# One-hot gate matrices stored by pairs of tokens instead of by eights

## The chip, the cores and the metric

One NeuronCore of a Trainium2 chip runs the whole program; the other cores are idle. The metric is the device time of one execution in microseconds (us), median of three executions. TensorE (PE; its weight loads are listed as PEld), VectorE (DVE), ScalarE (ACT), GpSimd (POOL) and the DMA queue engine (SP) run side by side, each taking its own instructions strictly in order and waiting on semaphores of the others.

## What is computed

One decoder layer over 512 tokens of width 1024: an attention head group, a state-space head group, and at the end an expert mixer, which is where this change lies. For each token 8 heads choose 16 of 16,384 experts each; expert number e = 128·i1 + i2:

```
eidx = take_along_axis(i1 * 128 + i2, sel)      # 8 heads x 16 experts per token
gate = softmax(top)
hid  = einsum('bcd,bchkd->bchk', xb, u_tab[eidx])
act  = gelu(hid) * gate
out  = einsum('bchk,bchkd->bcd', act, v_tab[eidx])
```

Then a residual sum and a last RMS norm.

## The kernel before

The 512 tokens are four tiles of 128. Tiles 0 and 1 ("sparse") gather the rows of their chosen experts from memory, 128 rows at a time. Tiles 2 and 3 ("dense", together 256 tokens) don't gather: they go through all 16,384 experts in 128 blocks of 128 (`dense`, loop over j), multiply every expert with every token, and weight the result with a gate that is zero where the token did not choose the expert. That needs, for each of the 256 tokens, a 128 x 128 table of gates (i1 by i2).

**How a gate table is made.** `dtab` holds for each token, on 128 partitions (one for each of its 8 x 16 choices), four f16 numbers: i1, i2, the gate's high part and its low part. `gate_parts(c, t0, b0)` treats eight tokens t0 to t0+7 at once and one half c of the i2 values (JC = 64 of them). It has four parts, separated by `yield`:

1. DVE writes A: for every token a 128 x 128 one-hot matrix of i1 (128 x 1024 numbers on 128 partitions, f16).
2. DVE writes B0, the one-hot matrix of the half of i2 (128 x 512), and then B, which is B0 times the high part (q = 0) and B0 times the low part (q = 1), 128 x 1024 together.
3. PE: for each token two matmuls (q = 0 and 1) with A as stationary and B as moving operand, 64 columns each, summed into one PSUM bank: 16 weight loads and 16 matmuls for eight tokens.
4. ACT copies the bank (128 x 512) into the gate rows in SBUF.

So A is built as `[i1, token]` with the eight tokens innermost, and PE reads one token of it with a step of 16 bytes; B likewise. `io8` is the constant that DVE compares with: the numbers 0 to 127, each eight times.

**Where it runs.** 32 groups with c = 0 run ahead of the loop over j, by `gate_tokens`, right after the first block's `hi`, `lo`, `hid` and `gelu`. This text calls that stretch the gate stage. Its buffers come from six small slots, three for a group (B0, A, B), so that two groups can be under way. A slot's freeing order makes a group's B0 and A lie where A and B of the group two before it lay. The order of the instructions in this stretch is not written by hand: the builder's scheduler interleaves the groups with each other and with their neighbours. The 32 groups with c = 1 run inside the loop, one for every two blocks up to about block 62; there the order on DVE, ACT, PE and POOL is as written (`with ordered(...)`), and B0 lies in `junk`, which the next `dot` overwrites.

One block of the loop: `hi` (ACT) and `lo` (DVE) split the loaded expert rows into two parts; `hid` (24 matmuls of 256 columns) and `outp` (12 of 512) on PE; `gelu` and `acthi` on ACT; `gated` and `actlo` on DVE; and one step of tile 1's gather work (`dot` and `add` on DVE, 128 x 1024 each). All instructions pass through one recording helper, so the profile names line 134 for nearly all of them, and tiles have to tell them apart: `X` is the large SBUF arena, `XH`/`XL` the split tokens, `bank` a PSUM bank.

Of the kernel before, what the change touches and what calls it, by code (L numbers as in the profile page):

```python
# [15 lines left out]
F16 = mybir.dt.float16  # L16
# [3 lines left out]
ALU = mybir.AluOpType  # L20
# [11 lines left out]
JC = 64  # L32
# [111 lines left out]
def both(g1, g2, n):  # L144

    for x in g1:
        yield x
        for _ in range(n):
            next(g2, None)
    yield from g2  # L150
# [7 lines left out]
def paced(w, g):  # L158
    for _ in g:
        yield w  # L160
# [3 lines left out]
def hymba_kernel(ctx: ExitStack, tc: tile.TileContext, a, out, dbg=None):  # L164
    nc = tc.nc
    pins = set()
    V, S, G, PE = (Ordered(tc, e, n, pins) for e, n in ((nc.vector, "V"), (nc.scalar, "S"), (nc.gpsimd, "G"), (nc.tensor, "PE")))
# [22 lines left out]
    base = arena.tile([128, 32768], F32, name="X")  # L190
# [6 lines left out]
    def bank():  # L197
        return pool[0].popleft()

    def bfree(*bs):  # L200
        pool[0].extend(bs)
# [88 lines left out]
    def load_w(name, n, pref=(4, 5)):  # L290
        r = [M.L(pref) for _ in range(2)]
        for i in range(2):
            SP.dma_start(r[i].v([128, 4, n]), a[name][:, 4 * i:4 * i + 4])
        return r, lambda k: r[k // 4].v([128, 4, n])[:, k % 4]
# [7 lines left out]
    w2 = const("w2", [128, 2, 64])  # L302
    msl = M.L((3,))
    VC = msl.v([128, NT, 280])
    io8 = msl.v([128, 128, 8], F16)
    dtab = msl.v([128, 4, 256], F16, off=4480)
    cmpb = msl.v([128, NT, 2, 31], off=7040)
    SP.dma_start(cmpb, a["cmpb"])
# [272 lines left out]
    def proj_q(T, w, e):  # L581
        p = bank()
        proj(T, w, 512, p)
        qs, ts = M.S(), M.S()
        Q = qs.v([128, 8, 64])
        S.activation(qs.v([128, 512]), p, AF.Copy, scale=0.125)
        bfree(p)
        rope_apply(e, Q, 8, ts.v([128, 8, 16]), ts.v([128, 8, 16], off=512), rope[:, T, 0], rope[:, T, 1])
        p = bank()
        for i in range(4):  # L590
            PE.transpose(b3(p, 128)[:, i], Q[:, 2 * i:2 * i + 2].rearrange("p h d -> p (h d)"), ident)
        S.activation(qT[T], b3(p, 128), AF.Copy)
        bfree(p)
        M.free(qs, ts)
        tap(f"qT{T}", qT[T])

    def proj_k(T, w, e):
        p = bank()
        proj(T, w, 512, p)
        ks_, ts = [M.S(), M.S()], M.S()  # L600
        KD = [k.v([128, 4, 2, 64]) for k in ks_]
        for i in range(2):
            S.activation(KD[i][:, :, 0], b3(p, 64)[:, 4 * i:4 * i + 4], AF.Copy)
        S.activation(KD[1][:, :, 1], b3(p, 64)[:, 4:8], AF.Copy)
        bfree(p)
        rope_apply(e, KD[0][:, :, 0], 4, ts.v([128, 4, 16]), ts.v([128, 4, 16], off=512), rope[:, T, 0], rope[:, T, 1])
        S.activation(KD[0][:, :, 1], KD[0][:, :, 0], AF.Copy)
        t0 = T * 128
        for n in (1, 0):
            p = bank()  # L610
            pv = b3(p, 128)
            for i in range(4):
                PE.transpose(pv[:, i], KD[n][:, i].rearrange("p u d -> p (u d)"), ident)
            if n == 0:
                S.activation(KT[:, :, t0:t0 + 128], pv, AF.Copy)
            else:
                S.activation(CTv[0:64, :, t0:t0 + 128], pv[0:64], AF.Copy)
                S.activation(CTv[64:128, :, max(t0 - 1, 0):t0 + 127], pv[64:128, :, 1 if T == 0 else 0:], AF.Copy)
            bfree(p)
        M.free(*ks_, ts)  # L620

    def proj_c(T, w):
        p = bank()
        proj(T, w, 280, p)
        S.activation(VC[:, T], p[:, 0:280], AF.Copy)
        bfree(p)
# [3 lines left out]
    def gates(T0, T1):  # L630

        g = gts[:, T0:T1]
        S.activation(g, VC[:, T0:T1, 256:280].rearrange("p t (h b) -> p t h b", b=3), AF.Tanh, scale=0.5)
        V.tensor_scalar(g, g, 1.0, 0.5, op0=ALU.add, op1=ALU.mult)
# [535 lines left out]
    def row(r):  # L1170
        return base[:, 2048 * (4 + r):2048 * (5 + r)]
# [13 lines left out]
    def gate_parts(c, t0, b0):  # L1185

        al, bl = M.S(), M.S()
        A = al.v([128, 128, 8], F16)
        B0 = Slot(b0, "B").v([128, JC, 8], F16)
        B = bl.v([128, 2, JC, 8], F16)  # L1190
        tsl = slice(t0, t0 + 8)
        V.tensor_tensor(A, io8, dtab[:, 0, None, tsl].to_broadcast([128, 128, 8]), op=ALU.is_equal)
        yield
        V.tensor_tensor(B0, io8[:, c * JC:(c + 1) * JC], dtab[:, 1, None, tsl].to_broadcast([128, JC, 8]), op=ALU.is_equal)
        sh = [128, 2, JC, 8]
        V.tensor_tensor(B, B0[:, None].to_broadcast(sh), dtab[:, 2:4, None, tsl].to_broadcast(sh), op=ALU.mult)
        yield
        b = bank()
        pg = b[:, 0:8 * JC].rearrange("p (t j) -> p t j", t=8)
        for t in range(8):  # L1200
            for q in range(2):
                PE.matmul(pg[:, t], A[:, :, t], B[:, q, :, t], start=(q == 0), stop=(q == 1))
        yield
        q, t1 = t0 // 32, t0 % 32
        if c == 0:
            dst = base[:, 2048 * 4:2048 * 12].rearrange("p (r q j t) -> p t r q j", r=8, q=8, j=8)[:, t1:t1 + 8, :, q]
            S.activation(dst, pg.rearrange("p t (r j) -> p t r j", j=8), AF.Copy, scale=1.0 / GSC)
        else:
            S.activation(row(q - 1).rearrange("p (j t) -> p t j", j=JC)[:, t1:t1 + 8], pg, AF.Copy, scale=1.0 / GSC)
        bfree(b)  # L1210
        M.free(al, bl)
# [247 lines left out]
    def rest():  # L1459

        for T in range(1, NT):
            proj_k(T, wk2[1], G)
            if T == 1:
                hold.close()
            yield W["k"]
        M.free(*wk2[0])
        wc2 = load_w("wC", 280, (0, 4))
        w_q = load_w("wA", 512, (0, 4))
        for T in range(1, NT):
            proj_c(T, wc2[1])  # L1470
            yield W["c"]
        M.free(*wc2[0])
        gates(1, NT)
        for T in range(1, NT):
            proj_q(T, w_q[1], G)
            yield W["q"]
        M.free(*w_q[0])
        zpool.__exit__(None, None, None)
        fpool = ctx.enter_context(tc.tile_pool(name="xnsplit", bufs=1, reuse_waits="tile"))
        XH = fpool.tile([128, 8, 256], F32R, name="XH")  # L1480
        XL = fpool.tile([128, 8, 256], F32R, name="XL")
        compress(0, 31, kcF, vcF)
        M.free(csl)
        yield W["cmp"]
        yield from paced(W["att"], attention(1))
        yield from paced(W["glu"], glu_out(1, 4))
        M.free(ysl, *gll)
        XHf = XH.bitcast(F32)

        def mixed(xns, dst):  # L1490

            yield from mix_out(xns, wo)
            for T, xn in xns.items():
                def w(n, p):
                    S.activation(dst(T, n), p, AF.Copy)
                    if T in DENSE:
                        i = DENSE.index(T)
                        ks, ts = slice(4 * n, 4 * n + 4), slice(128 * i, 128 * i + 128)
                        S.activation(XH[:, ks, ts], p, AF.Copy)
                        V.tensor_tensor(XL[:, ks, ts], p, XHf[:, ks, ts], op=ALU.subtract)  # L1500
                transpose_xn(xn, w)
                yield

        wo = load_wo()
        x1 = [M.S() for _ in range(2)]
        X1 = [x.v([128, 4, 128]) for x in x1]
        yield from paced(W["mix"], mixed({1: half(l01[1], 0)}, lambda T, n: X1[n]))
        rl = []

        def later():  # L1510
            for T in (2, 3):
                yield from attention(T)
            M.free(ksl, qsl)
            rl.extend([M.L((4, 5)), M.L((4, 5))])
            yield from mixed({T: half(rl[0], T - 2) for T in (2, 3)},
                             lambda T, n: rl[1].v([128, 8, 256])[:, 4 * n:4 * n + 4, 128 * T - 256:128 * T - 128])
            for i, T in enumerate(DENSE):
                SP.dma_start(hsave[i], xs[T])

        yield from paced(W["r1"], both(route([Topk(1)], lambda k: X1[k // 4][:, k % 4], 128), later(), NR))  # L1520
        M.free(rl[0], *x1)
        state["p1"] = True
        yield from paced(W["route"], route([Topk(2), Topk(3)], lambda k: rl[1].v([128, 8, 256])[:, k], 256))
        M.free(rl[1])
        G.iota(io8, pattern=[[1, 128], [0, 8]], base=0, channel_multiplier=0, allow_small_or_imprecise_dtypes=True)
        M.group()
        state["x"] = (XH, XL)

# [120 lines left out]
```

## Time and profile before

| | |
|---|---|
| three executions | 1695.72, 1697.57 (median), 1702.57 us |
| the profiled execution | 1694.28 us, of which the span from first to last instruction 1692.5 us |
| PE, busy share of the span | 87% (weight loads 69%) |
| DVE | 86% |
| ACT | 51% |
| POOL | 29% |
| mean granted TensorE clock | 0.903 of full speed |

Matmuls are pipelined, so PE's busy share is not the share of its peak. The average hides stages with different limits: the gate stage lies at about 800 to 900 us of the span, the part of the loop with gate groups at 904 to 1312 us, the rest of the loop without them up to about 1670 us.

### The profile page before, as it was taken

The numbers are of one execution on the slowest core, as the hardware profiler recorded it, in microseconds if no ns is written. First come the engines' busy times: TensorE is split into PE (matmuls) and PEld (weight loads), VectorE is DVE, ScalarE is ACT, GpSimd is POOL, SyncE is SP. The second block draws the span as 40 slices with busy tenths as digits, with TensorE's granted clock in tenths as the row PEclk, the third lists the DMA queues.
The fourth block names the chain that finished last, engine by engine and source line by source line (L and its number), as shares of the span: only waits on it lengthen the run. The fifth ranks groups of instructions, "written<-read, shape, count | busy, mean of one in ns | idle before, by whom it ended". The sixth has DMA issues, their size and how long they took to land.

```text
span 1692.5 us, 24254 instructions
## 1 busy us (share of the span) xinstructions
PE 1476.3 (87%) x8348; PEld 1171.8 (69%) x8348; DVE 1456.8 (86%) x3305; ACT 861.9 (51%) x2069; POOL 490.8 (29%) x383
## 2 busy tenths in 40 slices
PE   5687891989486899987669999999999999999996
PEld 2366570555254467643668999999999999999995
DVE  8986199878998648998657999999999999999998
ACT  1345324554454722555435555555555555555653
POOL 6423014745433000333001222222222333333331
PEclk9887896869676899999558999999999999999998
DMA  6221597979988443888404888888888999999994
GB/s 251 100 100 66 184 346 277 367 264 382 343 299 339 166 152 106 331 296 320 163 1 168 322 324 324 316 317 326 322 324 311 373 375 375 382 375 376 374 378 180
DMA packets 88967, 469.47 MB, mean 277 GB/s; under 512 B 10252, under 2 KB 10892, under 8 KB 50700
## 3 DMA queue, kind: packets, MB, share of 16 engines
q0 software_dynamic: 37152, 268.98, 41.5%
q1 hardware_dynamic: 51692, 198.94, 32.6%
q8 instruction: 65, 1.06, 0.2%
q14 instruction: 58, 0.48, 0.1%
HBM read 464.74 MB, written 3.15 MB: 276 GB/s over the span
## 4 chain that ended last, share of the span: by engine, by line
PE 49%; DVE 2%; DMA 1%; ACT 0%; issue 0%; SPq 0%; ACTq 0%
PE bank L134 49%; DVE X L134 2%; DMA raw<-in_uvt 1%; DVE f_r L134 0%; DVE lo L134 0%; ACT junk L134 0%; DVE junk L134 0%; ACT hi L134 0%; ACT raw L134 0%; ACT gt L134 0%; ACT dg L134 0%; ACT act L134 0%; ACT X L134 0%; DVE act L134 0%; DVE f_s L134 0%
## 5 line engine op out<-in xcount | busy, mean ns | idle before, releaser
L134 POOL DMA_INDIRECT X<-in_uv,eidx x256 | 398.9, 1558 | 1032.0 <-DVE X L134 804.8
L134 PE MATMUL bank<-X 128*128 128x64 f16 (+10 forms) x1768 | 311.3, 335 | 55.9 <-DVE X L134 47.0
L134 ACT ACTIVATE X<-bank 128x256 f32<-128x256 f32 (+4 forms) x423 | 219.5, 523 | 268.5 <-PE bank L134 221.9
L134 PE MATMUL bank<-hi,act 128*128 128x512 f32 x1024 | 299.7, 394 | 0.0
L134 PE MATMUL bank<-XH,hi 128*128 128x256 f32 x1024 | 288.8, 282 | 2.3 <-ACT hi L134 2.3
L134 DVE TENSOR_TENSOR X<-X 128x256 f32<-128x256 f32 (+13 forms) x579 | 231.1, 427 | 68.9 <-PE bank L134 40.8
L134 PE MATMUL bank<-XH,lo 128*128 128x256 f32 x1024 | 287.7, 281 | 0.5 <-DVE lo L134 0.5
L134 PE MATMUL bank<-XL,hi 128*128 128x256 f32 x1024 | 287.4, 281 | 0.0
L134 DVE CUSTOM_DVE_ANT_0 junk<-X 128x1024 bf16<-128x1024 f32 x206 | 251.0, 1219 | 10.0 <-DMA X<-in_uv,eidx 7.3
L134 DVE SCALAR_TENSOR_TENSOR X<-X,act 128x1024 f32<-128x1024 f32 x179 | 228.8, 1278 | 4.4 <-ACT act L134 4.4
L134 ACT ACTIVATE gt<-hid 128x1 f32<-128x1 f32 x384 | 63.7, 197 | 301.0 <-DVE hid L134 300.2
L134 DVE TENSOR_TENSOR lo<-raw,hi 128x1024 fp32r<-128x1024 f32 x172 | 209.8, 1220 | 1.4 <-ACT hi L134 1.4
L134 PEld LDWEIGHTS bank<-hi,act 128*128 128x128 f32 x1024 | 184.0, 189 | 32.0
L134 ACT ACTIVATE hi<-raw 128x1024 fp32r<-128x1024 f32 x172 | 181.4, 1054 | 47.1 <-PE bank L134 42.2
L134 PEld LDWEIGHTS bank<-XH,hi 128*128 128x128 f32 x1024 | 193.8, 189 | 7.5 <-ACT hi L134 2.6
L134 PEld LDWEIGHTS bank<-XL,hi 128*128 128x128 f32 x1024 | 193.3, 189 | 4.9
L134 PE MATMUL bank<-X,X 128*128 128x128 f32 (+7 forms) x888 | 179.4, 377 | 19.2 <-ACT X L134 11.1
L134 PEld LDWEIGHTS bank<-XH,lo 128*128 128x128 f32 x1024 | 194.1, 190 | 0.8 <-DVE lo L134 0.8
L134 PEld LDWEIGHTS bank<-X,X 128*128 128x128 f32 (+4 forms) x888 | 122.0, 198 | 64.0 <-issue 29.9
L134 PE MATMUL bank<-lo,act 128*128 128x512 f32 x512 | 159.0, 392 | 0.4 <-DVE lo L134 0.4
L134 PEld LDWEIGHTS bank<-X 128*128 128x128 f32 (+3 forms) x744 | 116.6, 195 | 60.1 <-issue 35.3
L134 PEld LDWEIGHTS <-X 128*128 128x128 f16 x1024 | 121.5, 147 | 33.2 <-DVE X L134 27.4
(202 smaller groups left out, 1845.6 us busy)
## 6 DMA issues: line engine op xcount, KB each, us to landing
raw<-in_uvt SPq DMA_DIRECT2D x172, 512.0 KB, 7.7
X<-in_uvt SPq DMA_DIRECT2D x84, 512.0 KB, 5.3
X<-in_wq SPq DMA_DIRECT2D x24, 1024.0 KB, 5.7
X<-in_wo SPq DMA_DIRECT2D x8, 1024.0 KB, 5.2
X<-in_x SPq DMA_DIRECT2D x8, 512.0 KB, 3.2
X<-in_wB SPq DMA_DIRECT2D x4, 1024.0 KB
X<-in_wA SPq DMA_DIRECT2D x4, 1024.0 KB
X<-in_w SPq DMA_DIRECT2D x4, 1024.0 KB, 5.0
```

Of the source, the lines that this page charges most:

```text
L134: ins = self.last = f(*args, **kw)
```

## The change

A is built as `[pair of tokens, i1, token of the pair]`, so that one token's column step is 4 bytes; B0 and B likewise. The constant shrinks from eight copies to two (`io2`). The table operand is read as two numbers, repeated for all i1, then the next two. B's product is issued as two instructions of 128 x 512, one for each q, in place of one of 128 x 1024. Matmuls, their order inside a group, PSUM and the copy out are the same.

```diff
-    io8 = msl.v([128, 128, 8], F16)
+    io2 = msl.v([128, 128, 2], F16)
...
-        A = al.v([128, 128, 8], F16)
-        B0 = Slot(b0, "B").v([128, JC, 8], F16)
-        B = bl.v([128, 2, JC, 8], F16)
-        tsl = slice(t0, t0 + 8)
-        V.tensor_tensor(A, io8, dtab[:, 0, None, tsl].to_broadcast([128, 128, 8]), op=ALU.is_equal)
+        A = al.v([128, 4, 128, 2], F16)
+        B0 = Slot(b0, "B").v([128, 4, JC, 2], F16)
+        B = bl.v([128, 2, 4, JC * 2], F16).rearrange("p q u (j t) -> p q u j t", t=2)
+        tab = [dtab[:, i, t0:t0 + 8].rearrange("p (u t) -> p u t", t=2) for i in range(4)]
+        sh = [128, 4, 128, 2]
+        V.tensor_tensor(A, io2[:, None].to_broadcast(sh), tab[0][:, :, None].to_broadcast(sh), op=ALU.is_equal)
         yield
-        V.tensor_tensor(B0, io8[:, c * JC:(c + 1) * JC], dtab[:, 1, None, tsl].to_broadcast([128, JC, 8]), op=ALU.is_equal)
-        sh = [128, 2, JC, 8]
-        V.tensor_tensor(B, B0[:, None].to_broadcast(sh), dtab[:, 2:4, None, tsl].to_broadcast(sh), op=ALU.mult)
+        sh = [128, 4, JC, 2]
+        V.tensor_tensor(B0, io2[:, None, c * JC:(c + 1) * JC].to_broadcast(sh), tab[1][:, :, None].to_broadcast(sh), op=ALU.is_equal)
+        for q in range(2):
+            V.tensor_tensor(B[:, q], B0, tab[2 + q][:, :, None].to_broadcast(sh), op=ALU.mult)
         yield
...
-                PE.matmul(pg[:, t], A[:, :, t], B[:, q, :, t], start=(q == 0), stop=(q == 1))
+                PE.matmul(pg[:, t], A[:, t // 2, :, t % 2], B[:, q, t // 2, :, t % 2], start=(q == 0), stop=(q == 1))
...
-        G.iota(io8, pattern=[[1, 128], [0, 8]], base=0, channel_multiplier=0, allow_small_or_imprecise_dtypes=True)
+        G.iota(io2, pattern=[[1, 128], [0, 2]], base=0, channel_multiplier=0, allow_small_or_imprecise_dtypes=True)
```

Because the scheduler sees one more instruction in each group, the built order moves too. On DVE in the gate stage, before (128x1024 with a wait for PE is an A, 128x512 a B0, 128x1024 that waits for DVE alone a B; "x2" is two in a row):

```order
L134 TENSOR_TENSOR X<-X 128x1024 [waits DVE_49,PE_49]
L134 TENSOR_TENSOR X<-X 128x512
L134 TENSOR_TENSOR X<-X 128x1024 [waits DVE_49,PE_49]
L134 TENSOR_TENSOR X<-X 128x512
L134 TENSOR_TENSOR X<-X 128x1024 [waits DVE_49] x2
```

and with the change (128x512 that waits for PE is a B0, the two others the halves of B):

```order
L134 TENSOR_TENSOR X<-X 128x512 [waits PE_49]
L134 TENSOR_TENSOR X<-X 128x1024 [waits PE_49]
L134 TENSOR_TENSOR X<-X 128x512 [waits DVE_49]
L134 TENSOR_TENSOR X<-X 128x512
L134 TENSOR_TENSOR X<-X 128x512 [waits PE_49]
```

Before, two groups are interleaved: A and B0 of the one, A and B0 of the other, then both B; the five rows are the repeating unit of two groups. Now the unit is one group, its four instructions in a row, and the fifth row is the next group's B0; this holds for groups 9 to 31 of the 32.

On PE where the first block's `hid` begins, before (`bank_85` is `hid`'s bank):

```order
L134 MATMUL bank_85<-XH,hi_5429 128x256 [waits Activation_49]
L134 MATMUL bank_85<-XL,hi_5429 128x256
L134 MATMUL bank_85<-XH,lo_5430 128x256 [waits DVE_49]
L134 MATMUL bank_85<-XH,hi_5429 128x256
L134 MATMUL bank_85<-XL,hi_5429 128x256
```

and with the change:

```order
L134 MATMUL bank_85<-XH,hi_5429 128x256 [waits Activation_49]
L134 MATMUL bank_85<-XL,hi_5429 128x256
L134 LDWEIGHTS X [waits DVE_49]
L134 MATMUL bank_84<-X 128x64 [waits DVE_49]
L134 LDWEIGHTS X
L134 MATMUL bank_84<-X 128x64 [waits DVE_49]
```

One gate group, the fifth (group 4), has moved from behind `hid` of the first block to between its second and third matmul, where PE waits for `lo`.

On DVE in the loop, at the first group that runs there, before:

```order
L134 TENSOR_TENSOR X<-X 128x1024 [waits PE_49]
L134 TENSOR_TENSOR junk<-X 128x512
L134 TENSOR_TENSOR X<-junk,X 128x1024 [waits DVE_49]
L134 ISA junk,hid<-X 128x1024 [waits DMASW7_49,DVE_49]
L134 ISA hid 128x1
```

and with the change:

```order
L134 TENSOR_TENSOR X<-X 128x1024 [waits PE_49]
L134 TENSOR_TENSOR junk<-X 128x512
L134 TENSOR_TENSOR X<-junk,X 128x512 [waits DVE_49]
L134 TENSOR_TENSOR X<-junk,X 128x512
L134 ISA junk,hid<-X 128x1024 [waits DMASW7_49,DVE_49]
L134 ISA hid 128x1
```

Here nothing moves: B's one instruction has become two, and `dot` (ISA) stands behind the second.

## Rows read from the trace of the kernel before

**Rows 1.** The chain of work that ended last, in order of time: start in us, length in us, engine, what it writes, instructions. The end of the gate stage and the loop.

```profile
886.38 1.64 DVE X L134 x3
888.07 4.12 PE bank L134 x32
...
904.36 766.81 PE bank L134 x5048
```

**Rows 2.** Busy time by stretch: the stretch and its length, then PE, PEld, DVE, ACT and POOL busy (instructions), granted TensorE clock, DMA share and GB/s. The gate stage, the loop with gate groups, the loop without.

```profile
818.30:899.90 81.60, 57.20 (x450) 53.58 (x449) 43.66 (x79) 30.05 (x28) 0.00 (x0) 0.52 0.07 24
904.40:1311.50 407.10, 407.10 (x2729) 375.21 (x2729) 387.15 (x528) 230.93 (x403) 92.94 (x62) 1.00 0.87 317
1318.00:1680.00 362.00, 358.94 (x2303) 325.40 (x2301) 346.67 (x455) 211.06 (x386) 124.88 (x62) 1.00 0.94 362
```

**Rows 3.** The timeline inside the gate stage: start, length, engine, operation, count, and in brackets the idle time before and what ended it.

```profile
829.90 4.10 PE L134 MATMUL bank<-X 128*128 128x64 f16 x32 [1.73 <-DVE X L134]
...
832.08 1.03 DVE L134 TENSOR_TENSOR X<-X 128x1024 f16<-128x1024 f16 x2 [1.64 <-PE bank L134]
834.04 2.23 DVE L134 TENSOR_TENSOR X<-X 128x1024 f16<-128x1024 f16 x4 [0.93 <-PE bank L134]
835.73 4.09 PE L134 MATMUL bank<-X 128*128 128x64 f16 x32 [1.73 <-DVE X L134]
```

**Rows 4.** The timeline of PE in the loop: a gate group, and what follows it.

```profile
930.66 2.15 PE L134 MATMUL bank<-X 128*128 128x64 f16 x16
932.56 0.71 PE L134 MATMUL bank<-hi,act 128*128 128x512 f32 x2
```

**Rows 5.** The timeline of DVE over the same two blocks, from one `dot` (CUSTOM_DVE_ANT_0) to the one two blocks later; 128x1024 f16 is A, junk 128x512 is B0, the one from junk is B.

```profile
929.87 1.22 DVE L134 CUSTOM_DVE_ANT_0 junk<-X 128x1024 bf16<-128x1024 f32 x1
...
934.25 0.42 DVE L134 TENSOR_TENSOR act<-X,act 128x256 fp32r<-128x256 f32 x1 [0.47 <-ACT act L134]
...
935.72 0.68 DVE L134 TENSOR_TENSOR X<-X 128x1024 f16<-128x1024 f16 x1
936.32 1.22 DVE L134 CUSTOM_DVE_ANT_0 junk<-X 128x1024 bf16<-128x1024 f32 x1
...
937.47 1.22 DVE L134 TENSOR_TENSOR lo<-raw,hi 128x1024 fp32r<-128x1024 f32 x1
938.82 0.43 DVE L134 TENSOR_TENSOR X<-X 128x256 f32<-128x256 f32 x1
...
941.83 0.42 DVE L134 TENSOR_TENSOR junk<-X 128x512 f16<-128x512 f16 x1
942.29 0.69 DVE L134 TENSOR_TENSOR X<-junk,X 128x1024 f16<-128x1024 f16 x1
943.01 1.23 DVE L134 CUSTOM_DVE_ANT_0 junk<-X 128x1024 bf16<-128x1024 f32 x1
```

**Rows 6.** Groups of instructions by shape over the whole span: matmuls and weight loads with 16-bit operands. Count, busy us, mean ns of one, idle time before. The f16 ones are the gate groups' (operands with a step of 16 bytes), the bf16 ones read an identity and a mask without gaps.

```profile
L134 PE MATMUL bank<-X 128*128 128x64 f16 x1024 | 134.3, 302 | 26.8 <-DVE X L134 26.8
L134 PE MATMUL bank<-c_maskb,identb 128*128 128x128 bf16 x64 | 16.2, 254 | 0.0
L134 PEld LDWEIGHTS <-X 128*128 128x128 f16 x1024 | 121.5, 147 | 33.2 <-DVE X L134 27.4 <-issue 4.5
L134 PEld LDWEIGHTS <-identb 128*128 128x128 bf16 x64 | 6.3, 99 | 36.6 <-issue 35.5
```

**Rows 7.** The fastest long run of load-and-matmul pairs: its timeline row, the length of one (min/median/max in ns), and, as in rows 2, the stretch around it.

```profile
357.73 1.13 PE L134 MATMUL bank<-kcF,X 64*128 64x31 f32 x16
...
L134 PE MATMUL bank<-kcF,X x48: 246/272/418, 357.7 to 530.3; 64*128 64x31 f32 x48
...
357.70:359.20 1.50, 1.50 (x20) 1.20 (x19) 0.55 (x2) 1.49 (x2) 0.00 (x0) 1.00 0.63 120
```

**Rows 8.** Groups of DVE instructions by shape, as in rows 6. With `mx` one operand is a single number read 31 times before the next (the second of the two 128x248 rows has no such operand); with `c_peT` one operand lies in single numbers with gaps.

```profile
L134 DVE TENSOR_TENSOR X<-X 128x1024 f16<-128x1024 f16 x96 | 64.9, 687 | 40.9 <-PE bank L134 40.8
L134 DVE TENSOR_TENSOR X<-X 128x512 f16<-128x512 f16 x32 | 13.3, 418 | 0.0
L134 DVE TENSOR_TENSOR X<-X 128x512 f32<-128x512 f32 x12 | 7.9, 689 | 0.2
L134 DVE TENSOR_TENSOR X<-X,c_peT 128x496 f32<-128x496 f32 x4 | 4.1, 1039 | 0.0
L134 DVE TENSOR_TENSOR X<-X,mx 128x248 f32<-128x248 f32 x6 | 2.4, 400 | 0.0
L134 DVE TENSOR_TENSOR X<-X,X 128x248 f32<-128x248 f32 x3 | 1.2, 405 | 0.0
```

**Rows 9.** The timeline around the beginning of the gate stage and its end: ACT's `hi` of the first block, the first and third matmul of its `hid`, DVE's `lo` of the second block, the first gate groups behind `hid`, and the matmul that follows the last gate group.

```profile
811.65 1.06 ACT L134 ACTIVATE hi<-raw 128x1024 fp32r<-128x1024 f32 x1 [4.56 <-DMA raw<-in_uvt]
812.75 0.58 PE L134 MATMUL bank<-XH,hi 128*128 128x256 f32 x1 [2.33 <-ACT hi L134]
...
814.01 0.58 PE L134 MATMUL bank<-XH,lo 128*128 128x256 f32 x1 [0.46 <-DVE lo L134]
...
818.20 1.22 DVE L134 TENSOR_TENSOR lo<-raw,hi 128x1024 fp32r<-128x1024 f32 x1
818.34 4.09 PE L134 MATMUL bank<-X 128*128 128x64 f16 x32
...
899.91 0.56 PE L134 MATMUL bank<-XH,hi 128*128 128x256 f32 x1
```

## Prediction

> **What bounds the kernel now.** I read the chain of waits first, to see which engine carries the time around the gates [rows 1]. In the gate stage DVE and PE take turns in it; from 904.36 us on it is PE alone. So two stages have to be costed, each by its own limit.
>
> Second, busy time by stretch [rows 2]. In the gate stage (818.3 to 899.9 us, 81.6 us long) no engine is full: PE 57.2 us, DVE 43.7. In the loop with gate groups PE is busy for all of 407.1 us, which hold 31 pairs of blocks with one group each: 13.13 us for a pair. DVE is close behind with 387.2. In the later loop, without gates, PE is busy for 358.9 of 362.0 us; nothing is touched there, and I leave it as it is.
>
> Third, the timeline inside the gate stage shows why nobody is full [rows 3]. PE does two groups in 4.10 us, then idles for 1.73 until DVE has written the next B; its next run begins 5.83 us after the last. DVE waits 1.64 us and then 0.93 us for PE. It is a ring: DVE writes A and B0 of two groups, but both B come last, so PE gets nothing until all six are done, and DVE may not write the next A before PE has read the slots. The turn costs 5.83 / 2 = 2.9 us per group, although PE needs only some 2 and DVE less.
>
> Fourth, what the matmuls themselves cost. Thirty-two load-and-matmul pairs take 4.10 us [rows 3]; less the 0.30 us of a single matmul [rows 6], (4.10 - 0.30) / 31 = 0.123 us from one pair to the next. In the loop (2.15 - 0.30) / 15 = 0.123 us too [rows 4]. [...] A spacing that stays the same while the clock doubles is not made by the array. What the two stretches share are the operands with a step of 16 bytes. Among the groups by shape, the f16 matmul of 64 columns takes 302 ns where a bf16 one of 128 columns without gaps takes 254, and the f16 load 147 where the bf16 load takes 99 [rows 6]. I read this as: the reading of spaced operands bounds these pairs.
>
> **The change part by part.**
>
> *Spacing of the pairs.* No row has f16 operands with a step of 4 bytes. Upper bound: today's 0.123 us. Lower bound: the fastest long run of pairs, (1.13 - 0.27) / 15 = 0.057 us, at clock 1.00 [rows 7]; at clock 0.5 the same pair may take twice that, 0.114. I take 0.06 in the loop, by the row without gaps, and 0.06 to 0.114 in the stage. [...]
>
> *DVE per group.* In the loop A starts at 935.72 and what follows it at 936.32: 0.60 us [rows 5]. A record of 512 is 687 - 418 = 269 ns shorter [rows 8], so an instruction of 512 takes 0.33 to 0.34 from its start to the next. The new group is A, B0 and two halves of B: 0.60 + 3 x 0.34 = 1.62 us. This assumes that DVE keeps its f16 rate with the new table operand, two f16 (one 4-byte word) read again and again before the next two. The nearest row: `mx`, one number read 31 times, costs 400 ns where the same shape without it costs 405 [rows 8]. So nothing is added; the other bound is a rival below.
>
> *The gate stage.* In the new order a group's four instructions stand in a row, and the next group needs only the slots of the group two before it. The ring is broken: DVE writes g+1 while PE does g, and the slower of the two sets the pace. Where it starts: the first block's `hid` begins at 812.75 after a wait for DMA, and runs until 818.34 [rows 9]; group 4 now runs inside it, about 1.9 us [rows 4] less the 0.46 us that PE waits for `lo` there, so PE is free at some 819.8 with 27 groups left. DVE ended `lo` of the second block at 818.20 + 1.22 = 819.4 [rows 9]; about 2 us of gate work now stand ahead of it (estimate from the order and the 1.62), so 821.3, with 25 groups left to write. If DVE sets the pace: 821.3 + 25 x 1.62 + 0.5 for one hand-over + 1.1 for PE's last group = 863.4. If PE sets it, with 0.114 x 16 = 1.82 us: 819.8 + 27 x 1.82 = 869. The stage now ends at 899.91 [rows 9]. Gain 31 to 37; I take **36**.
>
> *The loop with gate groups.* Nothing moves in the order. PE gets shorter by 16 x (0.123 - 0.06) = 1.0 us in a pair: 13.13 - 1.0 = 12.1. DVE is next: from one `dot` to the `dot` two blocks later is 943.01 - 929.87 = 13.14 us [rows 5]. Idle in it are 0.47 before the gelu product and 0.13 before the 128x256 product at 938.82 (937.47 + 1.22 = 938.69), so 12.53 are work by the records, 12.37 by start to start. The split adds a fixed cost: B0 to B takes 942.29 - 941.83 = 0.46 now and B to `dot` 943.01 - 942.29 = 0.72, 1.18 together; afterwards 0.46 + 0.34 + 0.45 = 1.25, that is +0.07. So DVE needs 12.44 to 12.60, and becomes the bound. A queue that becomes the bound rarely loses all its waits, so I take 12.57: 0.56 x 32 groups = **18 us**, with 10 (a third of the room lost to remaining waits) to 22 around it. DMA covers it: 317 GB/s become 330, and 362 are held in the later stretch [rows 2]. With a pair spacing of 0.09 PE needs 12.6, and the result is the same; only above that does PE bind again.
>
> *At nothing.* The smaller constant: GpSimd writes it far ahead of its first use. ACT's copy out stays, and ACT is busy for 30 of the stage's 81.6 us [rows 2], so it has room for the faster pace. The number of matmuls, loads and PSUM banks stays.
>
> Sum: 36 + 18 = 54 us off. The profiled execution's 1694.28 becomes about 1640. The median of the three runs stands 3.3 us above it: 1697.57 - 54 = **1643.6, say 1643**. The case's own range: stage 31 to 37, loop 10 to 22, so 41 to 59 off, 1638 to 1657, and 1632 if both DVE waits vanish and the stage's first hand-over with them.
>
> **The rivals.**
>
> *Only the order helps.* The pair spacing stays at 0.123, because something other than the step bounds it. For it: it is the same at both clocks, which any cost outside the array would give. Against: the bf16 rows. PE then sets the pace with 16 x 0.123 = 1.96 us a group: 819.8 + 27 x 1.96 = 872.7, gain 27, and the loop gains nothing since PE is full there. 1697.57 - 27 = **1671**. Chance 0.10.
>
> *DVE pays for each table word.* In `c_peT` single numbers with gaps are read: 1039 ns for 128x496, where 128x512 without takes 689; scaled, (1039 - 672) / 496 = 0.74 ns a read [rows 8]. If a new word of a broadcast counted like that, A (512 words) would cost 0.38 more and each of 512 numbers 0.19: a group 1.62 + 0.95 = 2.57. Stage: 821.3 + 25 x 2.57 + 1.6 = 887, gain 13. Loop: 12.52 + 0.95 = 13.47, 0.34 x 32 = 11 lost. Together -2: **1696**, no change. The `mx` row speaks against it. Chance 0.09.
> [...]
>
> *DVE falls to one number per step.* If the f16 rate itself needs long rows, DVE works as with 4-byte numbers: 1.22 us for 1024 [rows 5] in place of 0.687, 0.689 for 512 in place of 0.418 [rows 8]: 0.53 + 3 x 0.27 = 1.34 more per group, 2.96. Stage: 821.3 + 25 x 2.96 + 1.6 = 897, gain 3. Loop: 12.52 + 1.34 = 13.86, 0.73 x 32 = 23 lost. Slower by 20: **1718**. It decides once a group costs DVE over about 2.5 us, where the loop's loss outruns the stage's gain. For it: every f16 row of today has at least eight adjacent numbers in each operand. Against: the output and the one-hot operand still run without gaps, and the table's pair still fills a 4-byte word. Chance 0.06.
>
> **How the numbers follow.** The forecast case keeps 0.75. Faster by over 0.5% (8.5 us, about what a measurement of this kernel can tell from no change) are the forecast and the first rival: 0.85. Same 0.09, slower 0.06. The range 1632 to 1672 takes in the forecast case and the first rival, and leaves the two others out.
>
> **What would show it.** Right: the f16 loads near 100 ns and a group's 16 pairs near 1.2 us in the loop; A still near 690 and the halves near 418 ns; in the stage DVE's groups back to back at about 1.62 us and the loop's start near 864; in the loop a pair near 12.6 with DVE almost full and PE's idle time ended by DVE or ACT; later blocks unchanged. Wrong: f16 matmul runs that still take 2.1 us for 16 (first rival), A records of 1 us or more (second and third), or a loop pair at 13.1 with PE no longer full, which would mean a wait that I don't see.

## The result and the profile after

The median fell from 1699.67 us (four runs) to 1639.09 us (four runs, 1634.00 to 1641.89): a ratio of 0.9642, 95% interval 0.9607 to 0.9676. The forecast was 1643 us. The profiled execution took 1637.53 us against 1694.28, so 56.75 us less, where 54 were forecast; between the two medians it is 60.6. The kernel before, run again beside the experiments, had medians of 1694.55 to 1696.14 us, so 60.6 is probably some us too much.

Busy time by stretch after, columns as in [rows 2]: the gate stage, the loop with gate groups (from the first group's first matmul to the last one's), the loop without, and two short stretches for the clock.

```profile
823.20:866.50 43.30, 29.26 (x400) 23.12 (x401) 40.62 (x100) 25.44 (x24) 0.00 (x0) 0.52 0.11 32
1270.00:1630.00 360.00, 350.20 (x2248) 317.54 (x2246) 345.67 (x484) 208.32 (x379) 123.89 (x61) 0.99 0.93 358
870.63:1255.81 385.18, 373.70 (x2730) 336.16 (x2729) 383.07 (x559) 216.89 (x403) 138.23 (x62) 1.00 0.92 334
819.84:820.49 0.65, 0.65 (x18) 0.55 (x17) 0.54 (x4) 0.64 (x2) 0.00 (x0) 1.00 0.81 277
838.00:858.00 20.00, 14.88 (x203) 11.53 (x200) 20.00 (x50) 12.98 (x14) 0.00 (x0) 0.50 0.01 2
```

Against [rows 2] the bound has changed hands. In the stage DVE is busy for 20.00 of 20.00 us from 838 to 858. In the loop with gates DVE is busy for 383.07 of 385.18 us (99.5%; before 387.15 of 407.10), and PE, which was never idle there, now has 11.5 us free.

The chain that ended last shows the same, columns as in [rows 1]:

```profile
823.28 34.57 DVE X L134 x86
...
1239.46 1.61 DVE X L134 x2
1251.88 1.62 DVE X L134 x2
1256.15 358.26 PE bank L134 x2319
```

and its shares by line from 870.60 to 1256.15 us:

```profile
by line: DVE lo L134 32.6%; DVE X L134 30.7%; issue 17.5%; DVE junk L134 12.4%; DVE act L134 6.0%; DVE hid L134 0.7%; PE bank L134 0.0%
```

Before, PE carried it from 904.36 on; now DVE does until 1256.15, inside the last gate group, and PE only from there ("issue" is time between two instructions in which the engine waited for nothing that the profile shows).

Where the 56.7 us of span went, by marks that both traces have (us from the span's start, then the length of the stretch):

| mark | before | after | shorter by |
|---|---|---|---|
| first `hid` begins | 812.75 | 814.95 | -2.2 |
| second `hid` begins, the gate stage behind it | 899.91, 87.15 | 866.51, 51.56 | 35.6 |
| first gate group of the loop | 904.36, 4.45 | 870.63, 4.12 | 0.3 |
| last gate group of the loop | 1311.49, 407.13 | 1255.81, 385.18 | 21.9 |
| end of the span | 1692.5, 381.0 | 1635.8, 380.0 | 1.0 |

The first line is no effect of the change: the first `hid` waits for a DMA, and in the fourteen traces of this study it begins between 807.95 and 817.27 us without an order by layout.

PE in the gate stage and in the loop after, and DVE around one gate group of the loop, columns as in [rows 3]; the PEld row shows the loads of one group behind its first two:

```profile
823.20 35.26 DVE L134 TENSOR_TENSOR X<-X 128x1024 f16<-128x1024 f16 x87
838.88 1.29 PE L134 MATMUL bank<-X 128*128 128x64 f16 x16 [0.32 <-DVE X L134]
839.21 0.80 PEld L134 LDWEIGHTS <-X 128*128 128x128 f16 x14 [0.20 <-issue]
840.49 1.29 PE L134 MATMUL bank<-X 128*128 128x64 f16 x16 [0.32 <-DVE X L134]
...
883.05 0.95 PE L134 MATMUL bank<-X 128*128 128x64 f16 x16 [0.23 <-DVE X L134]
895.48 0.95 PE L134 MATMUL bank<-X 128*128 128x64 f16 x16 [0.23 <-issue]
...
906.97 0.42 DVE L134 TENSOR_TENSOR junk<-X 128x512 f16<-128x512 f16 x1
907.42 0.76 DVE L134 TENSOR_TENSOR X<-junk,X 128x512 f16<-128x512 f16 x2
908.22 1.22 DVE L134 CUSTOM_DVE_ANT_0 junk<-X 128x1024 bf16<-128x1024 f32 x1
```

A group of the stage now takes 840.49 - 838.88 = 1.61 us, and PE waits 0.32 us for DVE in each. In the loop a pair of blocks takes 895.48 - 883.05 = 12.43. The operations themselves, columns as in [rows 6]:

```profile
L134 PE MATMUL bank<-X 128*128 128x64 f16 x1024 | 60.3, 211 | 30.4 <-DVE X L134 17.5 <-ACT X L134 3.8 <-issue 2.0
L134 PEld LDWEIGHTS <-X 128*128 128x128 f16 x1024 | 49.3, 109 | 44.8 <-issue 24.9 <-DVE X L134 16.3 <-DVE f_s L134 2.0
L134 DVE TENSOR_TENSOR X<-X 128x1024 f16<-128x1024 f16 x64 | 43.8, 686 | 0.0
L134 DVE TENSOR_TENSOR X<-X 128x512 f16<-128x512 f16 x96 | 35.9, 420 | 2.8 <-PE bank L134 2.8
```

The 1024 f16 matmuls fill 60.3 us of PE where they filled 134.3 [rows 6]. DVE's instructions cost what they cost before, 686 against 687 and 420 against 418 ns [rows 8].

### The profile page after: what moved, and what is told of

It is laid out like the page before. It is cut to its first block, busy times and chain, and to the rows that moved or that the text cites. A ratio compares the mean times of both kernels' runs of the same rounds, so it can differ in the third digit from the quotient of the medians.

```text
span 1635.8 us, 24303 instructions
## 1 busy us (share of the span) xinstructions
PE 1408.2 (86%) x8348; PEld 1096.7 (67%) x8348; DVE 1453.2 (89%) x3369; ACT 846.3 (52%) x2069; POOL 537.4 (33%) x383
## 4 chain that ended last, share of the span: by engine, by line
DVE 44%; PE 33%; issue 12%; DMA 5%; ACT 3%; POOL 2%; SPq 0%; DVEq 0%; POOLq 0%; ACTq 0%
PE bank L134 33%; DVE X L134 25%; DVE lo L134 8%; DVE junk L134 7%; DMA X<-in_uv,eidx 4%; ACT X L134 2%; POOL X L134 2%; DVE act L134 1%; DMA raw<-in_uvt 1%; DMA X<-in_wq 1%; DVE nm L134 1%; DVE more L134 1%; DMA X<-in_x 0%; ACT gt L134 0%; DVE zT L134 0%
## 5 line engine op out<-in xcount | busy, mean ns | idle before, releaser
L134 POOL DMA_INDIRECT X<-in_uv,eidx x256 | 445.9, 1742 | 935.2 <-DVE X L134 689.4
L134 ACT ACTIVATE X<-bank 128x256 f32<-128x256 f32 (+4 forms) x423 | 213.9, 519 | 193.6 <-PE bank L134 147.0
L134 PE MATMUL bank<-X 128*128 128x64 f16 (+10 forms) x1768 | 238.9, 283 | 60.4 <-DVE X L134 38.4
L134 DVE TENSOR_TENSOR X<-X 128x256 f32<-128x256 f32 (+13 forms) x611 | 231.0, 411 | 25.3 <-ACT X L134 20.1
L134 PEld LDWEIGHTS bank<-lo,act 128*128 128x128 f32 x512 | 95.9, 188 | 22.7 <-DVE lo L134 0.8
```

The costliest lines, as they stand in the source:

```text
L134: ins = self.last = f(*args, **kw)
```

## The experiments

Theory: two things bounded the gate groups, the time that PE needs to read columns 16 bytes apart (122 ns from one pair to the next), and in the stage a ring between DVE and PE; with the change DVE is the bound everywhere that gates are made. Rivals: the order alone, or the split of B alone, brings the gain; another limit holds the loop.

**Only the split of B**, with eight tokens innermost as before.

```diff
-        V.tensor_tensor(B, B0[:, None].to_broadcast(sh), dtab[:, 2:4, None, tsl].to_broadcast(sh), op=ALU.mult)
+        for q in range(2):
+            V.tensor_tensor(B[:, q], B0, dtab[:, 2 + q, t0:t0 + 8]..., op=ALU.mult)
```

> Layout of before (step 16 bytes), B issued as two halves. The built order of the gate stage stays that of before, two groups interleaved, so the order does not come from the split. Theory (the step bounds the pairs of load and matmul, and the ring of two groups bounds the stage): pair spacing 0.123 us, stage 2.9 us a group, loop pair 13.13 us with PE full: time as before, 1698 within 5 us. Rival (the split into halves brings the gain by itself): 1640.

Measured: 1695.63 us against 1696.14, ratio 0.9993 (0.9968 to 1.0017). Stage 85.99 us, loop pair 13.13. The built order stayed that of before. So the section on the change was wrong in one point: the additional instruction alone does not move the order of the stage; the order moved only together with the new layout.

**Only the order**: the layout and the single B of before, but from the ninth group on DVE's order is pinned to one group after the other.

```diff
-        for t0 in range(0, 256, 8):
-            gate_tokens(0, t0)
+        for t0 in range(0, 64, 8):
+            gate_tokens(0, t0)
+        with ordered("V"):
+            for t0 in range(64, 256, 8):
+                gate_tokens(0, t0)
```

> Layout and single B of before, but from the ninth group on DVE's order in the gate stage is one group after the other. Theory: PE then sets the pace with 16 x 0.123 = 1.96 us a group instead of 2.91; 24 groups gain 23 us; the loop gains nothing because PE is full there: about 1676. Rival (the order brings nothing as long as the step is 16 bytes): 1698. Rival (the order brings all of the stage and the loop gains too): 1640.

Measured: 1672.50 us, ratio 0.9869 (0.9826 to 0.9913). The timeline of PE in the stage, and its busy time by stretch (columns as in [rows 2]):

```profile
823.83 50.05 PE L134 MATMUL bank<-X 128*128 128x64 f16 x400 [1.85 <-DVE X L134]
...
823.83:873.60 49.77, 49.77 (x400) 47.06 (x401) 41.14 (x72) 27.50 (x24) 0.00 (x0) 0.50 0.01 1
```

400 matmuls without a pause, 49.77 / 25 = 1.99 us a group: the ring is gone and PE sets the pace. The stage is 65.68 us long in place of 87.15. The loop pair stays at 13.13. In all the order alone gains 23.6 us on the before of its own session (1696.14).

**Only the layout**: the change, with the interleaving of two groups that before had pinned from the ninth group on.

```diff
+        with ordered("V"):
+            for t0 in range(64, 256, 16):
+                ...  # two generators: A, B0 of the one; A, B0 of the other; B of both
```

> Layout of the change (step 4 bytes), but from the ninth group on DVE's order in the gate stage is the interleaving of two groups that before had. Theory: the ring is back, but PE's part of it is short: 32 x 0.054 + 0.25 = 2.0 us and 1.73 of DVE, 3.7 us per two groups against 3.22 in the change: 12 x 0.5 = 6 us lost, about 1645, loop pair unchanged at 12.43. Rival (the order is what breaks the ring, so the stage goes back to 2.9 a group): 24 x 1.3 = 31 us lost, 1670.

Measured: 1637.14 us, ratio 0.9659 (0.9618 to 0.9700), no different from the change. Two rows of PE in the stage:

```profile
830.31 2.15 PE L134 MATMUL bank<-X 128*128 128x64 f16 x32 [1.54 <-DVE X L134]
834.00 2.14 PE L134 MATMUL bank<-X 128*128 128x64 f16 x32 [1.54 <-DVE X L134]
```

The ring is back, with 834.00 - 830.31 = 3.69 us for two groups, as worked out beforehand (3.7), against 3.22. That makes the stage 55.05 us, 3.5 more than the change's, not 6, because the change's own last three groups lose 0.8 us each (told under the gate stage below), and the total shows none of it: this run's first `hid` began 4.6 us earlier. So the size of the loss was expected too large and lies within what a run scatters.

The four stages together: before 87.15, order alone 65.68, layout alone 55.05, both 51.56. Neither part is worth a fixed sum; the second to come finds little left.

**The step.** By fours (8 bytes), by one token a row (2 bytes), and by pairs for one operand alone:

```diff
-        A = al.v([128, 4, 128, 2], F16)
+        A = al.v([128, 2, 128, 4], F16)      # fours; single: [128, 8, 128, 1]
...
# a_pairs: A [128, 4, 128, 2], B0 and B as before;  b_pairs: A as before, B0 and B by pairs
```

> Step of 8 bytes: tokens by fours, the same order of instructions as the change. [...] Rival (any step over 4 bytes costs in full): spacing 0.123 us, loop pair 13.13, stage 1.96 a group, 1671.

> Only A (the stationary operand, 128 columns to a load) lies by pairs; B0 and B keep the step of 16 bytes and B its one instruction. If the load sets the spacing (128 columns in 0.122 us, 0.95 ns a column) it falls to what the 64 moving columns need at that rate, near 0.06 us, and the loop pair to 12.4 us (about 1645 in all, by the order of the stage). If the moving operand sets it (1.9 ns a column), the spacing stays at 0.122 and the loop pair at 13.13 us.

> Only B0 and B (the moving operand, 64 columns to a matmul) lie by pairs; A keeps the step of 16 bytes. If the load sets the spacing it stays at 0.122 us, the loop pair at 13.13 us with PE full. If the moving operand sets it, it falls to 0.03 us in the loop and the time is near the change's, 1640.

> One token a row: columns 2 bytes apart, no gap; DVE's table operand is one f16 read again for all columns. PE's pair spacing should be the array's, near 0.03 us in the loop. For DVE: if a repeated 2-byte number costs its f16 rate, A takes 1.22 and 512 numbers 0.69 us, 1.34 more for a group: 25 x 1.34 in the stage and 32 x 1.34 in the loop, 76 us lost, about 1715. If it keeps the rate, A stays at 0.69 and the time at 1639. I hold the first for likelier, since the change kept two tokens together.

Measured, with the median distance from one f16 matmul's start to the next in the traces:

| step of A, of B | at clock 1.0 | at clock 0.5 | stage | loop pair | total |
|---|---|---|---|---|---|
| 16, 16 (before) | 122 ns | 122 ns | 87.15 us | 13.13 us | 1699.67 us |
| 4, 16 | 116 | 117 | 62.74 | 13.03 | 1667.41, one run |
| 16, 4 | 61 | 60 | 60.14 | 12.43 | 1646.18, one run |
| 8, 8 | 62 | 62 | 52.86 | 12.40 | 1639.76, ratio 0.9675 (0.9626 to 0.9723) |
| 4, 4 (the change) | 30 | 53 | 51.56 | 12.43 | 1639.09 |
| 2, 2 | 29 | 53 | 88.13 | 13.76 | 1720.67, ratio 1.0156 (1.0136 to 1.0175) |

(The stages of the two mixed layouts also differ in the order that the builder chose for them; the loop's order is the same in all rows.) One gate group of the loop on PE, in the order 4, 16, then 16, 4, then 8, 8 (2.15 us before, 0.95 with the change):

```profile
893.72 2.02 PE L134 MATMUL bank<-X 128*128 128x64 f16 x16
...
891.33 1.37 PE L134 MATMUL bank<-X 128*128 128x64 f16 x16
...
884.27 1.16 PE L134 MATMUL bank<-X 128*128 128x64 f16 x16
```

Each operand has its own time to be read. The row 4, 16 gives that of the moving one, 116 ns for 64 columns 16 bytes apart (1.8 ns each), the row 16, 4 that of the stationary one, 61 ns for 128 columns (0.5 ns each). With both at 16 bytes the pair takes 122, little more than the longer of the two. Half the step halves it, to 62, at both clock levels; for the fours I had put just that, 0.123 x 8 / 16 = 0.061 us, as an estimate, and the change's time, 1639 us within 5. At 4 bytes the distance follows the clock, 30 ns at a granted clock of 1.00 and 53 at 0.50, and a step of 2 bytes brings no more than 1 ns, so I take the array to be the limit there. My expectation that the load might be the limit was wrong; it is the moving operand. Nor had I expected the load's own 61 ns once the moving operand lies by pairs: I had put 0.03 us there. A step of 8 bytes does not reach the array's pace: at clock 1.00 it costs 62 ns where 4 bytes cost 30.

With fours PE is slower per group (1.42 us in the stage where the change has 1.29), but not slower than DVE with its 1.61, so the time is that of the change. With one token a row PE is as fast as in the change (29 and 53 ns) and DVE is not:

```profile
L134 DVE TENSOR_TENSOR X<-X 128x1024 f16<-128x1024 f16 x64 | 78.0, 1219 | 0.0
L134 DVE TENSOR_TENSOR X<-X 128x512 f16<-128x512 f16 x96 | 61.2, 686 | 2.4 <-PE bank L134 2.4
```

1219 and 686 ns where the change has 686 and 420: a table operand that repeats one f16 costs DVE its f16 rate, one that repeats two does not. This is the third rival's mechanism, with its sign, slower than before. It starts one step beyond the change.

**Which engine bounds the loop.** In the loop's gate groups DVE writes only the first half of B, and PE reads it twice, so that these gates hold their high part twice and their low part not at all; once on the change, once on before.

```diff
-        for q in range(2):
+        for q in range(1 if c else 2):
...
-                PE.matmul(pg[:, t], A[...], B[:, q, ...], ...)
+                PE.matmul(pg[:, t], A[...], B[:, 0 if c else q, ...], ...)
```

> The change, but in the loop's gate groups DVE writes only the first half of B, and PE reads that half twice (the low part of these gates is left out). PE's work is the same, DVE has one instruction of 128x512 less in a pair of blocks. Theory (after the change DVE is the loop's bound): pair 12.43 - 0.34 = 12.09 us, 32 x 0.34 = 11 us off, about 1628. Rival (PE, DMA or a wait holds the pair at 12.4): 1639.

> The same in the kernel before: in the loop B is one instruction of 128x512 in place of 128x1024, PE reads it twice. Theory (before the change PE was the loop's bound): pair 13.13 us as before, time as before, 1697 within 4. Rival (DVE was already the bound): 32 x 0.27 = 9 us off, 1688.

Measured: on the change 1628.11 us, ratio to before 0.9600 (0.9579 to 0.9621); on before 1694.25 against 1695.37, 1.0008 (0.9988 to 1.0028). Busy time in the loop with gates, first of the change without that half:

```profile
866.38:1240.02 373.64, 368.18 (x2730) 333.94 (x2730) 371.52 (x528) 217.24 (x403) 131.62 (x62) 1.00 0.95 344
```

and of before without it:

```profile
901.08:1308.12 407.04, 407.04 (x2731) 375.27 (x2729) 379.11 (x528) 230.83 (x403) 94.85 (x62) 1.00 0.87 317
```

After the change 0.34 us less of DVE shorten the pair by 0.37 (12.05 in place of 12.43, 373.64 / 31). Before it, 8 us less of DVE in the stretch shorten nothing; PE is full at 407.04. DMA moves 344 GB/s in the faster loop, so it was no limit at 334. At 12.05 us PE is busy for 98.5%, and the two engines are nearly even. The totals alone would not tell this run from the change (0.9579 to 0.9621 against 0.9607 to 0.9676); the loop pair does.

**Work for GpSimd.** If DVE is the bound, the second half of B could go to GpSimd, which has room. Three tries: in the loop; in the loop with B0 in room of its own and one block earlier; in the stage alone.

```diff
-            V.tensor_tensor(B[:, q], B0, ...)
+            (G if c and q else V).tensor_tensor(B[:, q], B0, ...)       # pool, pool_early
+            (G if c == 0 and q else V).tensor_tensor(B[:, q], B0, ...)  # pool_stage
...
-                    return gate_parts(1, 8 * g, junk.bitcast(F32)[:, 0:256])
+                    return gate_parts(1, 8 * g, msl.v([128, 256], off=512))  # pool_early, B0 and B in A's step
```

> The change, but in the loop's gate groups the second half of B is written by GpSimd, which is idle for two thirds of the loop. Theory (DVE is the bound, GpSimd has room): pair near 12.09 us as in the run without that half, about 1628. Rival (GpSimd's instruction is so long, or slows DVE's so much, that PE waits for it, or gathers are issued late): 1639 or slower.

Measured: 1664.83 us, ratio to before 0.9813 (0.9796 to 0.9830), 26 us slower than the change. GpSimd's half and the `dot` that follows:

```profile
909.79 1.05 POOL L134 TENSOR_TENSOR X<-junk,X 128x512 f16<-128x512 f16 x1
910.88 1.22 DVE L134 CUSTOM_DVE_ANT_0 junk<-X 128x1024 bf16<-128x1024 f32 x1 [1.13 <-POOL X L134]
```

`dot` overwrites `junk`, where B0 lies, so it waits 1.13 us for GpSimd: DVE saves 0.34 and stands for 1.1. PE too waits for GpSimd's half, 22 times and 1.0 us each from 900 to 1200 us. Loop pair 13.31.

> As the run in which GpSimd writes the second half of B in the loop, but without the two waits that run showed: B0 lies in room of its own, so that dot does not wait for GpSimd, and B0 and B are written one block earlier, so that PE does not. Theory (these two waits ate the gain, DVE is still the bound): pair 12.43 - 0.34 = 12.09 us, 32 x 0.34 = 11 us off the change, about 1628. Rival (GpSimd's own work next to DVE's costs DVE as much as it saves): 1639.

Measured: 1648.78 us, ratio 0.9724 (0.9699 to 0.9749), still 10 us slower than the change. The waits are gone, but `dot` has become longer (min/median/max ns of the 56 from 880 to 1240 us, then DVE's gate group and one `dot` with GpSimd beside it):

```profile
L134 DVE CUSTOM_DVE_ANT_0 junk<-X x56: 1206/1638/2610, 884.0 to 1237.2; 128x1024 bf16<-128x1024 f32 x56
...
914.95 1.47 DVE L134 TENSOR_TENSOR X<-X 128x1024 f16<-128x1024 f16 x3
916.10 1.21 POOL L134 TENSOR_TENSOR X<-X 128x512 f16<-128x512 f16 x1 [0.26 <-DVE X L134]
916.33 2.06 DVE L134 CUSTOM_DVE_ANT_0 junk<-X 128x1024 bf16<-128x1024 f32 x1
```

Of the 56, the 28 that overlap a GpSimd multiplication take 2.06 us in the median, the 28 others 1.21. A pair has one of the first kind: +0.85. DVE's gate group took 0.60 + 1.25 = 1.85 us in the change and takes 916.33 - 914.95 = 1.38 now, so -0.47. 12.43 + 0.85 - 0.47 = 12.81; measured 12.84. The rival was right.

> The change, but in the gate stage alone GpSimd writes the second half of B (the loop is that of the change). DVE's work for a group falls from 1.62 to 1.28 us, GpSimd's instruction takes 1.05, PE's run 1.29. Theory (DVE sets the stage's pace, and GpSimd lengthened only the f32 dot beside it, from 1.22 to 2.06 us, not the f16 instructions, 0.425): 1.3 us a group, 25 x 0.3 = 8 us off the change, about 1631. Rival (f16 instructions of DVE are lengthened beside GpSimd too, or its half comes late for PE): 1.6 us a group or more, 1639 or slower.

Measured: 1651.84 us, ratio 0.9768 (0.9732 to 0.9804), 13 us slower than the change.

```profile
L134 DVE TENSOR_TENSOR X<-X 128x512 f16<-128x512 f16 x64 | 47.3, 768 | 3.7 <-PE bank L134 3.7
L134 POOL TENSOR_TENSOR X<-X 128x512 f16<-128x512 f16 x32 | 43.6, 1364 | 35.3 <-DVE X L134 33.7 <-DVE f_r L134 1.6
```

The 768 ns are a mean of two kinds: the 37 instructions that no GpSimd multiplication overlaps take 0.41 us in the median, as ever, and the 27 that begin while one runs 1.26. GpSimd's half, and DVE's first half and next B0 beside and behind it:

```profile
840.66 1.36 POOL L134 TENSOR_TENSOR X<-X 128x512 f16<-128x512 f16 x1 [0.76 <-DVE X L134]
841.04 1.25 DVE L134 TENSOR_TENSOR X<-X 128x512 f16<-128x512 f16 x1
842.22 0.41 DVE L134 TENSOR_TENSOR X<-X 128x512 f16<-128x512 f16 x1
```

So one instruction in each group is 0.84 us longer, a group takes 2.11 us with DVE never idle, and the stage 64.33 us against 51.56; the rival was right again. A, during which GpSimd's instruction begins, keeps its 0.68 us, and GpSimd's takes 1.36 in place of 1.05. I had read the 0.425 us of the first try as no contention; there the two did not overlap. Beside GpSimd's multiplication both DVE instructions grow by about the same, whatever their own length: `dot` by 0.85 us, from 1.21 to 2.06, and the f16 one by 0.84, from 0.41 to 1.25. In nearly all of these pairs the instruction that begins second is the one that becomes longer. In one it is not: a `dot` that began 0.47 us before GpSimd's took 2.61 us. So which of the two is held up, and by what, is not settled.

None of these beats the change. The fours, and the pairs in the order of before, are as fast; shorter was only the loop of the run that leaves out the low part of the gates.

## Why the prediction was right

*What bounded the kernel.* Right in both stages. The run with the order alone shows the ring (2.9 to 1.99 us a group), the run of before without a half of B shows that DVE was no second bound of the loop, where PE is full.

*Spacing of the pairs.* The cause was right, the lower bound too high. It was put at 57 ns from the fastest long run in the trace [rows 7], and at 114 for the low clock; measured were 30 and 53 (row 839.21: (0.80 - 0.11) / 13 = 0.053 us at clock 0.50; row of 819.84 to 820.49: 16 pairs in 0.65 us, (0.65 - 0.21) / 15 = 0.029 at 1.00). The row taken as a bound was no bound: its matmuls are f32, and 57 ns for 31 columns is 1.8 ns a column, where the f16 ones now take 30 / 64 = 0.5. The error cost nothing, because DVE is the slower one in either case, as the fours with 62 ns show. The 53 ns at the low clock also settle that DVE, and not PE, paces the stage: 16 pairs need 0.85 us of the 1.61.

*DVE per group.* 1.62 us forecast, 1.61 measured; A and the halves kept their 687 and 418 ns. The row on `mx` had told the right way between the two bounds, but with some luck: it is an f32 row, of a type that takes 689 ns for 512 numbers where f16 takes 418 [rows 8], so it could not show whether f16 keeps its rate, and the run with one token a row shows that a single f16 read again and again does lose it (1219 ns for A in place of 686). For a pair that is only repeated the 686 ns for A show no added cost.

*The gate stage.* 36 us forecast; 33.4 by its end (899.91 to 866.51), 35.6 by its length, since it began 2.2 us late. The late start is also why DVE came to the 25 groups at 823.2 and not at 821.3. What was missing inside the stage is that the last three groups took 2.41 us each in place of 1.61, as they wait for the group directly before them:

```profile
859.08 1.79 DVE L134 TENSOR_TENSOR X<-X 128x512 f16<-128x512 f16 x4 [0.62 <-PE bank L134]
...
860.59 1.29 PE L134 MATMUL bank<-X 128*128 128x64 f16 x16 [1.12 <-ACT X L134]
863.00 1.29 PE L134 MATMUL bank<-X 128*128 128x64 f16 x16 [1.12 <-ACT X L134]
```

DVE writes B0 and A of such a group only when PE is reading, or has read, the group before, so the two take turns again. ACT, which the rows of PE name, releases a group's first matmul alone; the second starts at 860.92, after DVE's last half. That is 2.4 us which no step of the prediction held. The prediction's sum by DVE's pace, 863.4 - 812.75 = 50.65 us, still came near the measured 51.56, because the rest took 1.5 us less than in the sum. So the agreement there is in part luck.

*The loop.* 18 us forecast, 21.9 measured (31 x 0.705). The pair came to 12.43, below the range of 12.44 to 12.60 by a hair, where I had taken 12.57 because waits rarely vanish. Here both did: the gelu product and the 128x256 product no longer wait, since DVE now reaches them later than their operands do. The term B0 to `dot` is 908.22 - 906.97 = 1.25, as forecast.

*The rivals.* The order alone: 1671 forecast for it, 1672.5 when it was made (27 us of gain forecast, 23.6 measured), but in the change the spacing did not stay. A cost for each table word, and one number per step: DVE's rows exclude both for pairs (686 ns for A, 420 for a half). The run with one token a row shows that the last was priced fairly: 20 us slower forecast, 25.3 measured against its own before. Its terms fit less well than its sum: in the loop 31 x 0.63 = 19.5 us lost where 23 were forecast, and the stage 1 us longer where it was to be 3 shorter.

## What to carry to other kernels

Before you lay out small matrices for TensorE, divide a run of load-and-matmul pairs into distances and compare them at both clock levels: one that stays the same while the clock doubles, as the 122 ns did here, points away from the array, and one that follows the clock, as 53 and 30 ns did, towards it. Here it was the reading of the operands, and half the column step halved it (62 ns). The layout that suits TensorE best may cost VectorE its f16 rate (one repeated f16 did, with 1219 ns for 1024 numbers, two did not, with 686), so look for the step at which neither pays. When a bound is lifted, work out the second engine's full time without its waits: here the loop's gain ended there (12.43 us against 12.44 worked out), and moving work from it to GpSimd made things worse, first by waits for GpSimd (1.13 us a time), and without these because the two slowed each other (`dot` took 2.06 us beside GpSimd and 1.21 alone, GpSimd's multiplication 1.21 where it had taken 1.05).

## What the runs showed of the hardware

- The moving operand, f16, cost 1.8 ns a column at a step of 16 bytes (116 ns for 64); the stationary one 0.5 ns a column at 16 (61 ns for 128). With both at 8 bytes the pair took 62 ns. At 4 bytes the pair took 30 ns at a granted clock of 1.00 and 53 at 0.50.
- A DVE operand that repeats a single f16 took 1219 ns for 1024 numbers, one that repeats a pair 686.
- `dot`, 1.21 us alone, took 2.06 beside a GpSimd multiplication of 128x512 f16; a DVE multiplication of 512 f16 that began beside one went from 0.41 to 1.26 us, and the GpSimd one from 1.05 to 1.36.
